# Splitting w_out by half blocks inside the retention, on GpSimd's queue, with two rooms for the samples' keys, values and scores

## The chip, the cores and the metric

The kernel runs on one core of one Trainium2 chip. The metric is the device time of one execution in microseconds (us). A core has five engines with a sequencer each: PE multiplies matrices, DVE (VectorE) and ACT (ScalarE) work on tiles, POOL (GpSimd) does so too, and SP (SyncE) does little but issue transfers. DMA transfers can be issued from SP's, ACT's and POOL's queues. Each engine runs its own instructions in program order; what is ready further back in the row does not overtake.

## The reference, cut to what matters

One step of a hybrid decoder for a prompt of 1024 positions and for 8 samples of 8 positions each. Three branches are made from one normed input, gated, merged and multiplied by `w_out`:

```python
z = rms_norm(x, gain) @ w_in
o_a, s_ret_new = retention(rq, rk, rv, s_ret, pos0)           # 4 heads, chunks of 128 positions
b_a = (silu(rg) * o_a) @ w_br_a
o_b, pool_new = pool_mix(pu, pool_buf, pos0, w_pool, pool_scale)
b_b = (silu(pg) * o_b) @ w_br_b
o_c = nsa_attention(nq, cmp, sel, win, ...)                   # paged rows, window rows, compressed rows
b_c = (silu(ng) * o_c) @ w_br_c
merged = gates[:, :, 0] * b_a + gates[:, :, 1] * b_b + gates[:, :, 2] * b_c
y = x + merged @ w_out
return rms_norm(y, final_gain), new states and cache rows
```

The matmuls take float32 factors as two float16 halves (hi and lo), three products for one. `w_out` (1024x1024 float32, 4 MB) therefore has to be split into hi and lo before its product, which is the last large one of the kernel.

## The kernel before

The work is written as one program for one core, and a scheduler orders each engine's instructions before it runs, by its own timeline of costs; `self.behind()` gives a part lower priority, so that the scheduler lays it into gaps. The stages follow each other: the prompt's projections and attention, to about 520 us; the retention (`retention`), to about 740 us; the samples' attention (`sample_attention`) together with the pooling branch, to about 887 us; the output stage (`output`) with the branch products, the merge and the product with `w_out`, to the end.

**The retention** runs over 36 steps (4 heads by 9 pieces of positions). A step multiplies the input with a block of `w_in` (tile `z`, 24 matmuls of 512 columns), rotates it (`rot`, on DVE), splits it into halves (`rh`: ACT L1259, then the low half on POOL L1260), multiplies (`at`), masks and splits (`am`, then `ah` on ACT L1275 and `al` on DVE L1276), and multiplies again (`ro`, L1328 to L1330). ACT also makes `Sh` (L1347) from the state `S`, `vh` from `z`, `ob` with its row sums `rst`, and `oh`. POOL makes `rst` (L1300, L1301) and the low half of `ga` (L917). A generator of preparatory work for the samples, `prep`, is stepped once a step from the seventh on, behind everything else.

**The samples' attention** runs over four groups `tt` of two samples. For each sample POOL gathers rows of `cache_sel` and `cache_win` into a room `sraw`, ACT and DVE split them into `skd` and `svs`, PE makes scores `s1`, `s2`; DVE and ACT make the softmax in `sS` and `sst`; PE transposes `sS` (`ta` L1089, `tb` L1091), ACT and DVE split that (`sph` L1096, L1098 and `spl` L1097, L1099), PE multiplies with the values (`so`, L1108 and L1111), DVE gathers `soc` (L1114, L1115), PE transposes (`sto`, L1117). The tiles `svs`, `sks`, `sS` and `sst` have one room each, so a group's values and scores take the room of those of the group before.

**The pooling branch** lies between the groups. PE multiplies the input with blocks of `w_in` (tile `pj`, L309 to L311, 384 or 320 columns); ACT takes `pj` (`ue` L1423, `th` L1464), DVE makes `dd`, PE multiplies with `wpl` (`y`, L1467), and DVE and ACT make `gb` (L1468, L1472, L1473), hi and lo of the gated branch. `gb` is the left factor of the output stage's first matmuls `pb` (`branch`, L1642 to L1644).

**The split of w_out** (`out_weights`) is called after the pooling, in a pool of its own. For each of 8 blocks of 128 rows SP issues the load into `wr`, ACT makes `wh` (L222) and DVE makes `wl` (L223), both 128x1024, and SP issues two stores into `wod`, in DRAM. The two halves come from the helper `wsplit`, which also splits `w_in` (tiles `rwh`, `rwl`, `whi`, `wlo`). `wod` is read again only near the end, at 1121 us.

**The output stage** opens by laying rooms `T2`, `T3`, `T4` for factors of a Strassen product, loads them from `txd` and lays `T4a` for the first branch's weights (`store_pair`), which it loads on ACT's queue. The lines that the steps of the prediction turn on, besides those that the difference shows:

```python
with self.behind():
    self.sample_attention(sp, psb, pst)
next(pool, None)
self.out_weights(self.pool(es, "wout"))
...
if n > 5:
    with self.behind():
        next(prep, None)
```

## Time and profile before

| what | value |
|---|---|
| runs of the kernel before | 1311.88, 1307.58, 1310.80 us; median 1310.8 |
| the profiled execution | 1306.29 us; its span 1304.5 us, 1.8 us outside it |
| PE busy | 1251.3 us, 96% of the span |
| DVE, ACT, POOL busy | 912.2, 631.3, 525.2 us |
| matmuls | 10520 |

The span runs from the first to the last instruction that the profile records. A busy share is the time in which an engine worked on an instruction, and an idle stretch of PE is named by the tile it waited for. PEclk is the TensorE clock that was granted, as a share of full speed; it is 1.00 in most stretches and 0.50 in a few. Times of an execution are read on the profiled execution's own scale, which lies 4.5 us under the median of the three runs.

### The profile page before, as it was taken

To read this page: it belongs to the slowest core of one execution; us is meant where nothing else is said; L and a number is where in the kernel's file an instruction comes from. 1 tells how busy PE (TensorE), PEld (TensorE's weight loads), DVE (VectorE), ACT (ScalarE), POOL (GpSimd) and SP (SyncE) were. 2 spreads that over 40 slices of the span, in tenths; PEclk is the share of its full clock that TensorE was granted. 3 is DMA by queue.
4 is the path that set the end of the run, shared out by engine and by line. 5 is a ranking of instruction groups with operands and counts; after the bars stand their busy time and mean duration, and the time that the engine had idled before them with its cause. 6 is when DMAs were issued, how large, how long until landed. Compare 5 with 4: busy or idle time off the path is not lost. (4 is left out here: it accounts for less than half of the span.)

```text
span 1304.5 us, 27795 instructions
## 1 busy us (share of the span) xinstructions
PE 1251.3 (96%) x10520; PEld 850.6 (65%) x10520; DVE 912.2 (70%) x2288; ACT 631.3 (48%) x1474; POOL 525.2 (40%) x561
## 2 busy tenths in 40 slices
PE   7999899989999989999999999999999999999997
PEld 4555566767677764555655565657788888888643
DVE  6648635788777864766766668663698877578975
ACT  5633436667676763555554454433544333213331
POOL 1122013567676751445553550101743566323133
PEclk9999899999999999999999999998999999999998
DMA  7766623698899996243741278327542211543632
GB/s 251 182 133 149 149 66 86 99 147 146 164 173 205 192 207 174 58 124 104 173 139 35 85 202 264 77 76 255 180 130 58 58 49 55 175 145 114 227 96 97
DMA packets 324315, 179.24 MB, mean 137 GB/s; under 512 B 204433, under 2 KB 298609, under 8 KB 323764
## 3 DMA queue, kind: packets, MB, share of 16 engines
q1 hardware_dynamic: 283844, 137.83, 45.3%
q10 hardware_dynamic: 35600, 26.32, 6.8%
q0 software_dynamic: 4736, 13.31, 3.2%
q8 instruction: 82, 1.34, 0.4%
q14 instruction: 53, 0.43, 0.1%
HBM read 98.80 MB, written 33.25 MB: 101 GB/s over the span
## 5 line engine op out<-in xcount | busy, mean ns | idle before, releaser
L761 POOL TENSOR_TENSOR hl<-S,hl 128x640 f16<-128x640 f32 (+7 forms) x128 | 153.8, 1210 | 142.5 <-DVE hl L760 96.6
L309 PE MATMUL pj<-xh,whi 128*128 128x384 f16 (+1 forms) x480 | 153.0, 319 | 2.4 <-ACT ue L1423 2.1
L310 PE MATMUL pj<-xl,whi 128*128 128x384 f16 (+1 forms) x480 | 153.0, 319 | 0.0
L311 PE MATMUL pj<-xh,wlo 128*128 128x384 f16 (+1 forms) x480 | 152.8, 318 | 0.0
L288 PE MATMUL z<-rwh,xh 128*128 128x512 f16 x256 | 97.0, 379 | 0.0
L290 PE MATMUL z<-rwh,xl 128*128 128x512 f16 x256 | 97.0, 379 | 0.0
L289 PE MATMUL z<-rwl,xh 128*128 128x512 f16 x256 | 97.0, 379 | 0.0
L756 ACT ACTIVATE S<-S,nm 128x640 f32<-128x640 f32 (+7 forms) x128 | 93.7, 732 | 5.2 <-DVE hst L852 0.9
L311 PEld LDWEIGHTS <-wlo 128*128 128x128 f16 x672 | 66.1, 98 | 36.6 <-issue 1.3
L310 PEld LDWEIGHTS <-whi 128*128 128x128 f16 x672 | 66.1, 98 | 36.1 <-issue 4.9
L1572 DVE TENSOR_TENSOR q<-st,q 128x288 f32<-128x288 f32 (+1 forms) x168 | 70.3, 433 | 26.4 <-PE st L1563 25.3
L309 PEld LDWEIGHTS <-whi 128*128 128x128 f16 x672 | 66.1, 98 | 33.6 <-issue 1.3
L288 PEld LDWEIGHTS <-xh 128*128 128x128 f16 x448 | 45.3, 101 | 46.4 <-issue 7.2
L290 PEld LDWEIGHTS <-xl 128*128 128x128 f16 x448 | 43.9, 98 | 44.9 <-issue 0.7
L222 ACT ACTIVATE whi<-raw 128x1024 f16<-128x1024 f32 (+1 forms) x48 | 45.5, 948 | 57.0 <-PE pj L310 14.7
L289 PEld LDWEIGHTS <-xh 128*128 128x128 f16 x448 | 43.9, 98 | 42.1 <-issue 0.9
L755 ACT ACTIVATE hl<-S,nm 128x128 f16<-128x128 f32 (+7 forms) x64 | 49.1, 767 | 36.6 <-DMA pt<-hl 36.5
L1328 PE MATMUL o<-vst,pt 128*128 128x64 f16 x528 | 56.3, 193 | 10.7 <-DMA pt<-hl 10.6
L760 DVE CAST hl<-S 128x640 f16<-128x640 f32 (+4 forms) x64 | 33.2, 519 | 45.9 <-ACT S L756 16.2
L1260 POOL TENSOR_TENSOR rh<-rot,rh 128x256 f16<-128x256 f32 (+1 forms) x36 | 26.5, 735 | 89.1 <-ACT rh L1259 88.9
L310 PE MATMUL eg<-xl,whi 128*128 128x384 f16 (+1 forms) x192 | 61.5, 320 | 0.0
L309 PE MATMUL eg<-xh,whi 128*128 128x384 f16 (+1 forms) x192 | 61.5, 320 | 0.0
(511 smaller groups left out, 4056.0 us busy)
## 6 DMA issues: line engine op xcount, KB each, us to landing
raw<-w_in SPq DMA_DIRECT2D x26, 512.0 KB
raw<-w_in ACTq DMA_DIRECT2D x18, 512.0 KB
raw<-w_in SPq DMA_DIRECT2D x48, 128.0 KB
wad<-q ACTq DMA_DIRECT2D x21, 256.0 KB
txd<-rso SPq DMA_DIRECT2D x8, 544.0 KB
raw<-egd SPq DMA_DIRECT2D x16, 272.0 KB
s<-state_ret SPq DMA_DIRECT2D x16, 256.0 KB
o_ret_s<-s POOLq DMA_DIRECT2D x16, 256.0 KB
```

The costliest lines, as they stand in the source:

```text
L222: a = nc.scalar.activation(hi, raw, AF.Copy, scale=WS)
L288: nc.tensor.matmul(out, xh, hi[:, k, c0:c0 + n], start=(k == 0), stop=False)
L289: nc.tensor.matmul(out, xh, lo[:, k, c0:c0 + n], start=False, stop=False)
L290: self.marks["PE"] = nc.tensor.matmul(out, xl, hi[:, k, c0:c0 + n], start=False, stop=(k == 7))
L309: nc.tensor.matmul(out, hi[:, k, :], xh, start=(k == 0), stop=False)
L310: nc.tensor.matmul(out, hi[:, k, :], xl, start=False, stop=False)
L311: self.filled = nc.tensor.matmul(out, lo[:, k, :], xh, start=False, stop=(k == 7))
L755: nc.scalar.activation(hl[:, :w], s[:, d0:c1], AF.Exp, bias=nm[:, br:br + 1], scale=0.125)
L756: nc.scalar.activation(s[:, c0:c1], s[:, c0:c1], AF.Exp, bias=nm[:, br:br + 1], scale=0.125, accum_out=l[:, 0, br, r:r + 1])
L761: nc.gpsimd.tensor_tensor(hl[:, w:2 * w], s[:, d0:c1], hl[:, :w], op=ALU.subtract)
L1328: nc.tensor.matmul(out, lhs[0], rhs[0], start=start, stop=False)
L1572: nc.vector.tensor_tensor(out[:, c0:c0 + n], b, x[:, c0:c0 + n], op=ALU.add)
```

## The change

Three edits.

1. `out_weights` becomes a generator that the retention steps from its seventh step on, next to `prep` and behind everything else. One step issues the load of a block, the next splits it, so a block takes two steps, "half a block" each; the store of block k is issued immediately ahead of the load of block k+1, and the last store behind the eighth block. Loads and stores go on POOL's queue: 8 loads of 512 KB and, hi and lo lying side by side in one room, 8 stores of 512 KB in the place of 16. The rooms are those of the samples' rows, `sraw`, of which there are two and which stand empty in the retention: one holds the float32 block, the other, read as float16, its halves. ACT still makes the high half and DVE the low half. The pool `wout` goes away.
2. `svs`, `sks`, `sS` and `sst` have two rooms each.
3. In the output stage the first room `T4a` is laid ahead of `T2` to `T4`, and the loads of `T3` and `T4` are written behind the second pair's stores; SP's row has them directly behind the load of `T2` as before, and the order of PE's instructions behind the first `pb` is as before.

```diff
@@ -203,7 +203,6 @@
                 with self.behind():
                     self.sample_attention(sp, psb, pst)
                 next(pool, None)
-                self.out_weights(self.pool(es, "wout"))
         with ExitStack() as es:
             self.output(es)
         right.close()
@@ -1013,10 +1012,13 @@
         self.nc.gpsimd.indirect_dma_start(out=out, out_offset=None, in_=rows,
                                           in_offset=bass.IndirectOffsetOnAxis(ap=self.sidx[:, c:c + 1], axis=0))
 
+    def sraw(self, pool):
+        return pool.tile([P, 2, 2, 256], F32, tag="sraw", name=self.nm("sraw"), bufs=2)
+
     def sample_rows(self, pool, b):
 
         nc = self.nc
-        raw = pool.tile([P, 2, 2, 256], F32, tag="sraw", name=self.nm("sraw"), bufs=2)
+        raw = self.sraw(pool)
         for pg in range(2):
             self.gather(raw[:, pg, 0, :], "cache_sel", b * 2 + pg)
         nc.gpsimd.dma_start(raw[:, :, 1, :], self.d["cache_win"][0, b].rearrange("(q p) a g c -> p q (a g c)", p=P))
@@ -1034,8 +1036,8 @@
             for b in range(2):
                 bb = 2 * tt + b
                 raws.append(self.raw0[b] if tt == 0 else self.sample_rows(self.smc if tt == 2 else sp, bb))
-            vs = sp.tile([P, 2, 2, 2, 2, 2, 64], F16, tag="svs", name=self.nm("svs"))
-            ks = sp.tile([P, 2, 8, P], F16, tag="sks", name=self.nm("sks"))
+            vs = sp.tile([P, 2, 2, 2, 2, 2, 64], F16, tag="svs", name=self.nm("svs"), bufs=2)
+            ks = sp.tile([P, 2, 8, P], F16, tag="sks", name=self.nm("sks"), bufs=2)
             for b in range(2):
                 kd = sp.tile([P, 4, 2, 2, 64], F16, tag="skd", name=self.nm("skd"))
                 vo = vs[:, b].rearrange("p q r g a c -> p (q r) g a c")
@@ -1061,8 +1063,8 @@
                                                  tile_position=tp, **fl)
                             kn = self.kns[kr, br * 2 + g] if br < 2 else kcs[kr, g]
                             nc.tensor.matmul(s2[r, br, :], q, kn, tile_position=tp, **fl)
-            s = sp.tile([P, 704], F32, tag="sS", name=self.nm("sS"))
-            st = sp.tile([P, 24], F32, tag="sst", name=self.nm("sst"))
+            s = sp.tile([P, 704], F32, tag="sS", name=self.nm("sS"), bufs=2)
+            st = sp.tile([P, 24], F32, tag="sst", name=self.nm("sst"), bufs=2)
             for br in range(2):
                 nc.vector.tensor_tensor_reduce(out=s[:, br * 256:br * 256 + 256], in0=s1[:, br], in1=tcs, scale=1.0,
                                                scalar=LOW, op0=ALU.add, op1=ALU.max, accum_out=st[:, br:br + 1])
@@ -1162,7 +1164,7 @@
         nc.vector.memset(am, 0.0)
         env = (rope, mt, mts, rv, c2, seq16, qm, am, lg)
         steps = [(h, t) for h in range(4) for t in (0, 1, 2, 3, 8, 4, 5, 6, 7)]
-        prep = self.sample_prep(rp, psa)
+        prep, wout = self.sample_prep(rp, psa), self.out_weights()
         live = []
         for n in range(len(steps) + NSTAGE):
             z = None
@@ -1181,6 +1183,7 @@
             if n > 5:
                 with self.behind():
                     next(prep, None)
+                    next(wout, None)
             if n == len(steps) - 2:
                 with self.behind():
                     self.raw0 = [self.sample_rows(self.smc, b) for b in range(2)]
@@ -1501,17 +1504,23 @@
             self.wsplit(t[:, 0, :n], t[:, 1, :n], a)
             yield i, t[:, :, :n].rearrange("p a (k c) -> p a k c", c=P)
 
-    def out_weights(self, pool):
+    def out_weights(self):
+
 
         nc = self.nc
         self.wod = self.dr.tile([P, 8, 2, 1024], F16, name="wod")
-        for k in range(8):
-            raw = pool.tile([P, 1024], F32, tag="wr", name=self.nm("wr"), bufs=2)
-            nc.sync.dma_start(raw, self.d["w_out"][0][k * P:(k + 1) * P, :])
-            hl = [pool.tile([P, 1024], F16, tag="w" + x, name=self.nm("w" + x), bufs=n) for x, n in (("h", 2), ("l", 1))]
-            self.wsplit(*hl, raw)
-            for a in range(2):
-                nc.sync.dma_start(self.wod[:, k, a], hl[a])
+        hl = None
+        for k in range(9):
+            if hl is not None:
+                nc.gpsimd.dma_start(self.wod[:, k - 1], hl.rearrange("p (a c) -> p a c", a=2))
+            if k == 8:
+                return
+            raw, out = [self.sraw(self.smc).rearrange("p a b c -> p (a b c)") for _ in range(2)]
+            nc.gpsimd.dma_start(raw, self.d["w_out"][0][k * P:(k + 1) * P, :])
+            yield
+            hl = out.bitcast(F16)
+            self.wsplit(hl[:, :1024], hl[:, 1024:], raw)
+            yield
 
     def store_pair(self, wq, i, c0, c1, raw):
 
@@ -1658,11 +1667,12 @@
             wk = self.pool(e, "mwk", bufs=2)
             room = lambda p, tag, kh: p.tile([P, 2, kh, H], F16, tag=tag, name=self.nm(tag), bufs=1)
             xs = (self.xh, self.xl)
+
+            first = room(wk, "T4a", 4)
             tx = {x: room(wk, x, 4) for x in ("T2", "T3", "T4")}
             for a, x in enumerate(xs):
                 nc.sync.dma_start(x[:, 0:4, H:], self.txd[:, 0, a])
-            for i, x in ((2, "T2"), (1, "T3"), (3, "T4")):
-                nc.sync.dma_start(tx[x], self.txd[:, i])
+            nc.sync.dma_start(tx["T2"], self.txd[:, 2])
             rx = self.factors(lambda k, t, c0, n: [x[:, k, t * H + c0:t * H + c0 + n] for x in xs], 4, tx)
             jobs = [(w, C_MG + br * 1024, p) for br in (1, 2) for p in pairs] + [(d["w_br_a"][0], 0, pairs[0])]
             loads = chain((self.load_pair(wk, x, *[c + j * P for j in p]) for x, c, p in jobs),
@@ -1689,8 +1699,12 @@
                 if p == pairs[2]:
                     state.update(A=dict(next(loads)), more=iter(()))
                 if p < pairs[-1]:
-                    x = room(wk, "T4a", 4).rearrange("p a k c -> p (a k c)").bitcast(F32)
+                    x = first if p == pairs[0] else room(wk, "T4a", 4)
+                    x = x.rearrange("p a k c -> p (a k c)").bitcast(F32)
                     self.store_pair(wk, p[0], *[j * P + P for j in p], [x[:, o:o + 1024] for o in (0, 1024)])
+                if p == pairs[1]:
+                    for i, x in ((1, "T3"), (3, "T4")):
+                        nc.sync.dma_start(tx[x], self.txd[:, i])
                 for i, j in enumerate(p):
                     for s0, n in ((0, 352), (352, 192), (544, 352), (896, 192)):
                         pb = self.branch(ps, wb, lambda q: (self.gb, q), range(4 * i, 4 * i + 4), s0, n)
```

The following pieces show where that moves instructions. The names end in numbers of the build; L-numbers are lines of the kernel before or of the changed one, which lie some lines apart (L1259 of before is L1262 of the changed kernel).

PE at the seam from the samples' attention to the output stage, before: `so` and `sto` are the last group's products and transpose, `pb` are the output stage's first matmuls.

```order
L1108 MATMUL so_12055<-vcs,sph_12047 32x128
L1111 LDWEIGHTS spl_12048
L1111 MATMUL so_12055<-vcs,spl_12048 32x64
L1117 MATMUL sto_12107<-ident,soc_12104 128x128
L1642 LDWEIGHTS whi_12857
L1642 MATMUL pb_12905<-gb,whi_12857 128x352
```

The same seam in the changed kernel; `pj` is the pooling branch's last tile:

```order
L308 MATMUL pj_12773<-xh,whi_12703 128x320
L309 LDWEIGHTS whi_12703
L309 MATMUL pj_12773<-xl,whi_12703 128x320
L310 LDWEIGHTS wlo_12704
L310 MATMUL pj_12773<-xh,wlo_12704 128x320
L1470 MATMUL y_12801<-dd_12591,wpl 128x320
L1119 MATMUL sto_12156<-ident,soc_12153 128x128
L1651 LDWEIGHTS whi_12836
L1651 MATMUL pb_12883<-gb,whi_12836 128x352
```

Before, the last group's `ta`, `so`, `tb` and `sto` stand behind the last `pj`, with no other matmul among them. In the changed kernel the last `so` stands ahead of 22 matmuls of the last `pj`, and between that group's `ta`, `tb` and `so` stand further matmuls of `pj`; only `y` and `sto` are left between the last `pj` and the first `pb`.

ACT in the retention, before; `oh`, `ga`, `vh`, `ah`, `rh` and `Sh` are tiles of the retention's steps:

```order
L1304 ACTIVATE oh_8304<-ob_8201,rst_8200 128x256
L916 CAST ga<-to_8212 128x2x4x32
L1239 ACTIVATE rope<-rope,rv 128x1024 x2
L1250 ACTIVATE vh_8353<-z_8232 128x256
L1275 CAST ah_8277<-am_8275 128x128
L1259 CAST rh_8357<-rot_8348 128x256
```

The same place in the changed kernel:

```order
L1307 ACTIVATE oh_8310<-ob_8205,rst_8204 128x256
L915 CAST ga<-to_8216 128x2x4x32
L221 ACTIVATE sraw_8103<-sraw_8102 128x1024
L1242 ACTIVATE rope<-rope,rv 128x1024 x2
L1253 ACTIVATE vh_8363<-z_8238 128x256
L1278 CAST ah_8283<-am_8281 128x128
L1262 CAST rh_8367<-rot_8358 128x256
```

The split of a block (`sraw<-sraw`) now stands among these, eight times over, each 9 to 13 instructions of ACT behind the place at which the block's load was issued; before, the eight stood in ACT's row of the samples' stage, between `ue`, `skd` and `whi`.

POOL in the retention of the changed kernel; `wod<-sraw` is a store and `sraw<-w_out` a load:

```order
L1263 TENSOR_TENSOR rh_8367<-rot_8358,rh_8367 128x256
L916 TENSOR_TENSOR ga<-to_8315,ga 128x2x4x32
L1515 DMA wod<-sraw_8103 128x2048
L1519 DMA sraw_8330<-w_out 128x1024
L1303 TENSOR_TENSOR rst_8303<-rst_8303,half 128x1
L1304 TENSOR_TENSOR rst_8303<-rst_8303,rv 128x1
```

Such a pair of issues stands seven times in POOL's row, between the parts of the steps, with one load ahead of them and one store behind. SP's row loses 24 issues.

## Rows read from the trace of the kernel before

**Rows 1.** The page: its span, and busy time and share of each engine.

```profile
span 1304.5 us, 27795 instructions
...
PE 1251.3 (96%) x10520; PEld 850.6 (65%) x10520; DVE 912.2 (70%) x2288; ACT 631.3 (48%) x1474; POOL 525.2 (40%) x561
```

**Rows 2.** Busy time by stretches (clock and DMA share last).

```profile
core 0: us, PE busy (x) PEld busy (x) DVE busy (x) ACT busy (x) POOL busy (x), PEclk, DMA share, GB/s
545.00:660.00 115.00, 111.12 (x749) 64.18 (x744) 81.53 (x239) 64.14 (x180) 58.14 (x83) 1.00 0.52 135
...
790.00:800.00 10.00, 8.23 (x49) 5.07 (x47) 9.32 (x29) 6.19 (x16) 0.00 (x0) 1.00 0.84 263
...
870.00:881.10 11.10, 8.40 (x54) 5.43 (x52) 8.99 (x26) 5.25 (x16) 0.00 (x0) 1.00 0.35 106
881.10:891.30 10.20, 9.26 (x65) 6.00 (x64) 3.85 (x13) 2.61 (x7) 0.00 (x0) 0.50 1.02 387
...
900.00:1240.00 340.00, 339.53 (x2990) 276.18 (x2988) 263.79 (x459) 127.50 (x248) 142.85 (x109) 1.00 0.39 123
```

**Rows 3.** PE's waits from 740 to 900: total, times, longest.

```profile
PE pj L309 <- ACT ue L1423: 2.1, 1, 2.1
PE so L1108 <- ACT sph L1096: 1.5, 1, 1.5
PE tb L1091 <- DVE spl L1097: 1.2, 1, 1.2
```

**Rows 4.** PE's timeline at the seam: start, duration, instruction, wait.

```profile
876.57 0.30 PE L311 MATMUL pj<-xh,wlo 128*128 128x320 f16 x1
...
887.36 0.50 PE L1642 MATMUL pb<-gb,whi 128*128 128x352 f16 x1
887.65 0.50 PE L1643 MATMUL pb<-gb,whi 128*128 128x352 f16 x1
...
892.11 0.31 PE L1642 MATMUL pb<-gb,whi 128*128 128x352 f16 x1
892.25 0.31 PE L1643 MATMUL pb<-gb,whi 128*128 128x352 f16 x1
```

**Rows 5.** ACT's timeline about 798 us.

```profile
798.82 1.06 ACT L222 ACTIVATE wh<-wr 128x1024 f16<-128x1024 f32 x1 [1.17 <-DMA wr<-w_out]
799.79 0.47 ACT L1423 ACTIVATE ue<-pj 128x384 f32<-128x384 f32 x1
```

**Rows 6.** ACT's and DVE's timelines behind the last pj.

```profile
881.41 0.46 ACT L1472 CAST gb<-th 128x320 f16<-128x320 f32 x1
...
880.64 0.54 DVE L1468 SCALAR_TENSOR_TENSOR th<-y,psc,th 128x320 f32<-128x320 f32 x1
...
881.91 0.49 DVE L1473 TENSOR_TENSOR gb<-th,gb 128x320 f16<-128x320 f32 x1
```

**Rows 7.** Tile wr: w_out's split, and its engines' waits (us, times).

```profile
L222 ACT ACTIVATE wh<-wr x8: 1057/1057/1058, 768.9 to 807.1; 128x1024 f16<-128x1024 f32 x8
L223 DVE SCALAR_TENSOR_TENSOR wl<-wr,wh x8: 1205/1221/1226, 771.4 to 808.4; 128x1024 f16<-128x1024 f32 x8
...
  DMA wr<-w_out: 11.8, 6
```

**Rows 8.** PE's waits in the retention, 520 to 740.

```profile
PE ro L1328 <- ACT Sh L1347: 1.8, 1, 1.8
PE ro L1330 <- DVE al L1276: 1.5, 3, 0.7
PE ro L1328 <- ACT ah L1275: 1.0, 3, 0.4
```

**Rows 9.** ACT's longest waits in the retention, 545 to 665.

```profile
ACT oh L1304 <- POOL rst L1301: 19.9, 14, 2.6
```

**Rows 10.** POOL's issues into sraw (tile sraw), and stretch 770 to 790.

```profile
L1022 POOL DMA_DIRECT2D sraw<-cache_win x8: 773/777/802, 743.2 to 826.5; - x8
...
770.00:790.00 20.00, 20.00 (x159) 12.42 (x158) 19.46 (x39) 7.47 (x12) 10.12 (x9) 1.00 1.05 310
```

## Prediction

> **What bounds the kernel now.** I read the page's engine line first: PE is busy 1251.3 of 1304.5 us [rows 1], so the end moves only where PE's idle time or PE's speed moves. Then I read the stretches around the change [rows 2]. In the retention (545 to 660) PE idles 3.9 of 115 us; ACT is busy for 64.1, DVE for 81.5, POOL for 58.1. In the output stage (900 to 1240) PE idles 0.5 of 340. Between them three stretches stand out. In 790 to 800 PE idles 1.77 of 10 us. In 870 to 881.1 it idles 2.70. In 881.1 to 891.3 it idles 0.94, and the granted clock is 0.50, the lower of its two levels (1.2 against 2.4 GHz), so its 9.26 busy us are some 4.63 us of work at full speed.
>
> PE's waits in those stages name three causes [rows 3]: `pj` for ACT's `ue`, 2.1 us; `so` for ACT's `sph`, 1.5; `tb` for DVE's `spl`, 1.2. The timelines say what stands behind them. The last `pj` matmul starts at 876.57 and the first `pb` at 887.36, and at the seam the `pb` matmuls follow each other at 0.29 us, at 892.11 already without that stretching [rows 4]: the 1.47 and 1.23 us of idling come directly ahead of the fall of the clock. They are there because nothing else is left for PE to do while ACT and DVE make the last group's `sph` and `spl`. And ahead of the late `ue` ACT stood 1.17 us for the DMA of a `w_out` block and then split it for 1.06 us [rows 5]: that wait of 2.1 us is a cost of the split in its old place.
>
> **The change part by part.**
>
> *The seam.* In the new order the last group's `ta`, `tb` and `so` stand ahead of 22 matmuls of `pj` or between other `pj` matmuls, so the answers of ACT and DVE come while PE works. What goes: 2.70 us idle in 870 to 881.1, 0.94 idle in 881.1 to 891.3, and 9.26 / 2 = 4.63 us of lost clock, since with nothing idle ahead the clock has no cause to fall [rows 2]. Together 8.27 us. I put this down to the two rooms of `svs`, `sks`, `sS` and `sst`: without them the last group could not begin early. What is late next: the third group of `pb` (columns 544 on) needs the last piece of `gb`. That chain runs from the end of the last `pj`, 876.57 + 0.30 = 876.87, over `th` and `gb` on ACT and DVE to 881.91 + 0.49 = 882.40: 5.5 us [rows 4, 6]. Before, the products and the transpose covered it. Now `y`, `sto` and the first two groups of `pb` do. These last took 887.36 to 892.11, 4.75 us, most of it at half clock [rows 4]; at full clock I estimate 2.75, and with some 0.75 us for `y` and `sto` 3.5. But the old chain queued on ACT and DVE behind `sph`, `spl` and a block of weights. Its own steps are five of about half a microsecond (0.46, 0.54, 0.49 in [rows 6]), with hand-overs of up to 0.2 us between them (`th` ends at 881.18, `gb` starts at 881.41), so 2.4 to 3.5 us. The wait lies between 0 and 5.5 - 3.5 = 2.0 us; as the order still leaves one block's split among the steps, I take 0.35.
>
> *The split leaves the samples' stage.* Eight ACT instructions of 1057 ns and eight DVE instructions of 1221 ns go from there, with 11.8 us of ACT's standing for `wr` in six waits [rows 7]. Of all this PE felt one wait, 2.1 us [rows 3]; that is the gain. The 24 SP issues that go cost PE nothing, since no wait of PE there names them.
>
> *The split comes into the retention.* ACT gets 8 x 1.06 = 8.5 us, DVE 8 x 1.22 = 9.8 us [rows 7], in sixteen steps or some 100 us. On the stretch 545 to 660 that makes ACT 72.6 and DVE 91.3 of 115 us, 63 and 79%: there is room, and it costs nothing where the work slides into gaps. If the cover is gone, each split delays `ah`, `al` or `Sh`, for which PE already waits 1.0, 1.5 and 1.8 us [rows 8]. The bound from below is zero, or little more. The bound from above is that every block costs what the one at 798 us cost, 8 x 2.1 = 16.8 us, since a block is load wait plus split there too. The nearest row is the samples' stage as a whole, where eight such blocks cost PE 2.1 us [rows 3]; the retention hands over between engines more often, and I take 3 us. The order puts a split 9 to 13 ACT instructions, about one step of 6 us, behind its load's issue; the ACT waits for `wr` averaged 11.8 / 6 = 1.97 us at a DMA share of 0.84 [rows 2, 7], while the retention's stretch has 0.52. Loads of 4 MB and stores of 4 MB in 100 us add about 84 GB/s to 135, by which the share would come to some 0.84; `w_in`'s blocks come over the same engines, and later ones would show as ACT waiting for `raw`.
>
> *POOL's queue.* Eight loads and eight stores at the duration of a plain issue there, 0.78 us [rows 10], are 12.5 us; POOL goes from 58.1 to some 70.6 of 115 [rows 2]. Behind a store or load stand `rst`, the low half of `rh` and of `ga`. ACT's `oh` already waits 19.9 us in 14 waits for `rst` [rows 9], and none of PE's waits names `oh`, so a POOL some tenths later per step reaches PE only over the low half of `rh`, which precedes `at`. I book it within the 3 us. A store waits for both halves of its own block, made a step earlier; the loads behind it wait with it.
>
> *T4a first, T3 and T4 later in the text.* SP's and PE's rows keep their order there; the output stage from 900 on idles 0.5 of 340 us [rows 2], so I cost this at nothing. If `T4a` first moved the branch's weights earlier, PE still has no wait to lose.
>
> **The sum.** 8.27 + 2.1 - 0.35 - 3.0 = 7.0 us. The profiled execution took 1306.3 us, so 1299.3 on its own scale; the median of the three runs shown lies 4.5 above it, 1310.8, so the forecast is **1303.8 us**.
>
> **The rivals.**
>
> *The retention hides the split wholly.* ACT and DVE have more than a third and more than a fifth of the stretch free. Then the 3 us fall away: 1300.8.
>
> *The seam idles again, further on.* The chain to `gb` stays as long as it was, PE stands 2.0 us ahead of the third group of `pb`, and the clock falls as it did behind the 2.70 us. That takes 2.0 + 4.63 from the gain instead of 0.35: 10.4 - 6.6 - 3.0 = 0.8, 1310.0 us. For it speaks that the order leaves little between the last `pj` and `pb`; against it that PE's idling at 798 us, 2.1 us at one time, left the clock of its stretch at 1.00 [rows 2, 3].
>
> *The splits hold up the retention (slower).* ACT stands in its row for a block that is not yet there, and `ah`, `rh` and `Sh` stand behind it. At the price of the block at 798 us, 2.1 each [rows 3, 5], the change loses 16.8 and gains 10.0: 1317.6 us. It turns the sign from 10.0 / 8 = 1.25 us a block and is measurable from 1.74. For it speaks that ACT stood for six of eight blocks before [rows 7]; against it the step's distance of load and split, and a DMA share of 0.52.
>
> *POOL stalls on its issues.* Were an issue held for the length of a DVE instruction, up to 1.22 us [rows 7], sixteen would add 19.5 us to POOL; half of it on PE's path gives 9.8 us, 1310.6 us. Against it: while DVE was busy 19.46 of 20 us (770 to 790), issues of the samples' windows took 773 to 802 ns, hardly spread [rows 10]. The Trainium skill has the rule that speaks for this rival, under "SBUF — State Buffer", section "SBUF: two separate sides": descriptors of a DMA issued from GpSimd are written over a port pair that VectorE can hold locked, so that the transfer waits for the end of VectorE's instruction. In this trace the narrow spread does not bear it out for such issues.
>
> **How the numbers follow.** Chances: the forecast 0.50 (its own range 1300 to 1308), nothing lost in the retention 0.18, the seam again 0.15, the retention held up 0.12, POOL 0.05. A difference of 0.3%, 3.9 us, is about what a measurement of this kernel can tell from none, so faster means under 1306.9 and slower over 1314.7. Faster: 0.44 of the first (the upper end of its range lies within 0.3%), 0.18, and 0.02 of the milder form of the seam, 0.64. Same: the rest of the first 0.06, the seam 0.13, POOL 0.05, 0.24. Slower: 0.12. The range is 1299 to 1312: below it lies little, since the sum with nothing lost anywhere is 10.4; above it the held up retention.
>
> **What would show the steps right or wrong.** Right: PE's waits name no `so<-sph`, no `tb<-spl`, and no `pj<-ue` of 2 us, and the first `pb` follow at 0.15 us with a granted clock of 1.00. The split's ACT instructions lie between about 560 and 680 us, with short waits for the DMA. Wrong: a wait of over a microsecond ahead of `pb`, with the clock at 0.50 behind it; or PE's waits in the retention of well over 5 + 3 us, by `ah`, `al`, `rh` or `Sh`, with ACT standing for `sraw<-w_out`, or POOL's DMA issues taking over a microsecond. The prediction fails above all if the price of a block in the retention is not the 0.4 us that I took.

## The result, and the profile after

The changed kernel takes 1321.38 us in the median of 4 runs (1320.78 to 1322.44), the kernel before 1310.99 (4 runs): a ratio of 1.0086, with a 95% interval from 1.0062 to 1.011. It is slower, by some 10 us, where 1303.8 was forecast and 1312 was the upper end of the range. The profiled execution took 1321.12 us.

The page's span and engine line, which answer to [rows 1]:

```profile
span 1319.3 us, 27777 instructions
...
PE 1253.8 (95%) x10520; PEld 850.7 (64%) x10520; DVE 914.0 (69%) x2288; ACT 630.4 (48%) x1474; POOL 530.7 (40%) x577
```

PE does the same matmuls; 14.8 us more of span hold 2.5 more of busy time. To see where the rest lies I read five marks off PE's timeline in either trace (where the first `z`, the last `ro`, the first matmul of the third group of `pb`, the first `st` and the first `py` start; `st` and `py` are matmuls of the output stage), and took the stretches between them:

| stretch, us | before | after | difference |
|---|---|---|---|
| start to first `z` (code untouched) | 498.4 | 500.3 | +1.9 |
| first `z` to last `ro` (retention) | 257.5 | 267.8 | +10.3 |
| last `ro` to third group of `pb` (samples, seam) | 136.2 | 133.6 | -2.6 |
| third group of `pb` to first `st` (output's beginning) | 41.7 | 47.6 | +5.9 |
| first `st` to first `py` | 278.8 | 280.0 | +1.2 |
| first `py` to the span's end | 91.9 | 90.1 | -1.8 |

The first row is noise: over the thirteen profiled executions of this study that untouched stretch ran from 497.2 to 503.9 us. The last two rows nearly cancel. Three rows carry the result, and each went against the forecast: the retention lost over three times what was booked, the samples' stage gave back a quarter of the gain that was forecast for it, and the output stage, booked at nothing, lost 5.9.

**The retention.** PE's waits there, from 500 to 760 us (total, times, longest), against [rows 8]:

```profile
PE ro L1331 <- ACT ah L1278: 3.4, 1, 3.4
PE cms L989 <- DMA craw<-cache_cmp,idx: 2.2, 1, 2.2
...
PE ro L1331 <- ACT Sh L1350: 1.7, 1, 1.7
PE ro L1333 <- DVE al L1279: 1.4, 2, 1.1
```

ACT's waits for transfers, from 545 to 700 us:

```profile
ACT rwh L221 <- DMA raw<-w_in: 10.8, 6, 3.8
...
ACT sraw L221 <- DMA sraw<-w_out: 7.5, 4, 3.2
ACT whi L221 <- DMA raw<-w_in: 4.7, 2, 3.2
```

ACT's timeline through the longest of PE's waits, which ends in the `ro` of 587.81 us:

```profile
577.89 0.63 ACT L221 ACTIVATE rwh<-raw 128x512 f16<-128x512 f32 x1 [3.71 <-DMA raw<-w_in]
...
580.16 1.06 ACT L221 ACTIVATE sraw<-sraw 128x1024 f16<-128x1024 f32 x1
...
581.37 1.68 ACT L221 ACTIVATE rwh<-raw 128x512 f16<-128x512 f32 x3
...
586.93 0.63 ACT L221 ACTIVATE rwh<-raw 128x512 f16<-128x512 f32 x1 [1.42 <-DMA raw<-w_in]
587.47 0.28 ACT L1278 CAST ah<-am 128x128 f16<-128x128 f32 x1
```

The point of these rows is that `ah` stands in ACT's row directly behind `rwh`, the split of a piece of `w_in` (256 KB, brought by two loads of 128 KB), and that it is `rwh` that waits, for its own loads: 1.42 us here, 3.71 at the piece of 577.89. The wait for `w_out` itself (`sraw`) is there too, but it is not what stands ahead of this `ah`. What went out just ahead of that late piece are a store and a load of `w_out`, POOL's timeline, then SP's:

```profile
571.29 0.60 POOL L1515 DMA_DIRECT2D wod<-sraw  x1
571.88 0.54 POOL L1519 DMA_DIRECT2D sraw<-w_out  x1
```

```profile
572.80 0.55 SPq L274 DMA_DIRECT2D raw<-w_in  x1
```

The piece was used 5.1 us after this issue. Pieces of `w_in` come in only two bursts of eight in this window (issued from 565 to 584 and from 634 to 651 us), and a pair of `w_out` transfers meets each of them: in the second burst the pair went out at 635.22 and 635.82, and the piece issued at 636.37 was used 7.1 us later. In the kernel before, the pieces that ACT stood for were used 2.4 to 3.4 us after their issue. Step by step, by the starts of the `at` matmuls counted from the first `z`, the changed kernel is level with the one before up to the first burst, 3.3 us late behind it, 5.8 behind the wait for a gather (`cms`, at 629.8 us) and 10.3 behind the second burst; after that it loses nothing more. The loss has three places, not eight; at two of them it follows a late piece of `w_in`.

Busy time by stretches, with the granted clock ahead of the DMA share:

```profile
545.00:660.00 115.00, 104.94 (x700) 59.98 (x699) 79.52 (x225) 62.12 (x167) 59.64 (x91) 0.98 0.65 176
580.00:600.00 20.00, 16.61 (x128) 10.49 (x127) 14.04 (x34) 12.75 (x33) 11.63 (x17) 0.91 0.45 123
```

In 545 to 660 PE now idles 10.1 us where it idled 3.9 [rows 2], the DMA share is 0.65 against 0.52, and behind the wait of 3.4 us the clock fell to its lower level for some 3.5 us (0.91 in the mean of these twenty), and once more at 659.9 us; before, it was 1.00 throughout the retention.

**The samples' stage.** PE's waits from 760 to 920 us, against [rows 3]:

```profile
PE pt L1437 <- DVE tl L1434: 1.5, 1, 1.5
...
PE pb L1651 <- ACT gb L1475: 1.2, 1, 1.2
PE so L1110 <- ACT sph L1098: 0.9, 1, 0.9
PE ptb L1431 <- DVE win L1448: 0.5, 1, 0.5
PE tb L1093 <- DVE spl L1099: 0.5, 1, 0.5
```

The waits of [rows 3] at the seam and for `ue` are gone, and the clock is 1.00 where the first `pb` run. But new ones stand at other groups of samples, and `pb` waits 1.2 us for `gb`.

**The output's beginning.** ACT's timeline:

```profile
901.21 1.09 ACTq L1492 DMA_DIRECT2D T4a<-w_br_a  x2
...
914.60 1.15 ACT L221 ACTIVATE q<-T4a 128x512 f16<-128x512 f32 x2 [10.12 <-DMA T4a<-w_br_a]
915.65 0.30 ACT L1712 COPY mm<-pb 128x192 f32<-128x192 f32 x1
```

SP's timeline at the same time:

```profile
900.55 0.34 SPq L1675 DMA_DIRECT2D T<-txd  x1
901.14 0.81 SPq L1707 DMA_DIRECT2D T<-txd  x2
```

The same in the kernel before, ACT's timeline, then SP's:

```profile
888.44 1.02 ACTq L1489 DMA_DIRECT2D T4a<-w_br_a  x2
...
894.15 1.15 ACT L222 ACTIVATE q<-T4a 128x512 f16<-128x512 f32 x2 [1.53 <-DMA T4a<-w_br_a]
```

```profile
881.25 1.29 SPq L1665 DMA_DIRECT2D T<-txd  x3
```

Before, the three loads of `T` (1088 KB each) had 7.2 us of start over `T4a`, and `T4a` was used 5.7 us after its issue. Now they go out within the same microsecond and `T4a` is used 13.4 us after its issue. ACT stands for it 10.1 us, with the copies of `mm` behind it, and PE waits for `mm` from there on:

```profile
PE pb L1651 <- ACT mm L1712: 4.5, 6, 1.2
PE st L1570 <- ACT mm L1712: 1.6, 2, 0.9
PE pb L1651 <- ACT gb L1475: 1.2, 1, 1.2
```

(PE's waits from 900 to 960 us.) The kernel before has none of the first two, but for 0.5 us at one `st`. The time from the first load of `T` to the use of `T4a` hardly changed: 12.9 us before, 14.1 now. The 7 us in which PE idled and ran at half clock at the seam before were also the time in which that burst of loads was under way.

### The profile page after: what moved, and what is told of

Its sections match the earlier page's. It is cut to its first block, busy times and chain, and to the rows that moved or that the text cites. A ratio compares the mean times of both kernels' runs of the same rounds, so it can differ in the third digit from the quotient of the medians.

```text
span 1319.3 us, 27777 instructions
## 1 busy us (share of the span) xinstructions
PE 1253.8 (95%) x10520; PEld 850.7 (64%) x10520; DVE 914.0 (69%) x2288; ACT 630.4 (48%) x1474; POOL 530.7 (40%) x577
```

## The experiments

The theory after the traces: three separate costs. In the retention the transfers of `w_out` make the blocks of `w_in` late, and ACT's row passes that on; in the samples' stage the second rooms let a group's products move ahead of their factors; in the output stage `T4a` shares the DMA engines with the `T` loads. The rivals for the retention: the split's own work on ACT and DVE; ACT's standing for a block of `w_out`; POOL's queue. The table has each kernel's median, its ratio to the kernel before on the same chip with its interval, and three of the stretches from its profiled execution.

| kernel | median us | ratio | retention | samples, seam | output's beginning |
|---|---|---|---|---|---|
| before | | | 257.5 | 136.2 | 41.7 |
| the change | 1321.4 | 1.0086 [1.0062, 1.011] | 267.8 | 133.6 | 47.6 |
| e1, no split | 1313.3 | 1.0038 [1.0013, 1.0063] | 257.9 | 132.0 | 48.4 |
| e2, the work only | 1312.9 | 1.0030 [1.0013, 1.0046] | 257.9 | 132.7 | 48.4 |
| e3, the transfers only | 1321.6 | 1.0105 [1.0080, 1.0131] | 260.4 | 132.4 | 48.5 |
| e10, the same again | 1322.4 | 1.0079 [1.0052, 1.0105] | 265.5 | 130.8 | 48.4 |
| e4, the move only | 1324.7 | 1.0125 [1.0103, 1.0146] | 269.1 | 127.6 | 48.9 |
| e5, T4a first on SP | 1320.5 | 1.0053 [1.0031, 1.0075] | 269.8 | 134.0 | 43.2 |
| e6, no split, one room | 1308.8 | 0.9983 [0.9967, 1.0000] | 256.4 | 128.1 | 48.3 |
| e7, slow pace | 1312.1 | 1.0007 [0.9987, 1.0028] | 258.1 | 132.5 | 48.8 |
| e8, split late, one room | 1305.4 | 0.9952 [0.9931, 0.9973] | 258.6 | 128.9 | 43.4 |
| e9, slow pace, one room | 1306.5 | 0.9962 [0.9942, 0.9982] | 257.5 | 127.9 | 43.2 |
| e11, on SP's queue | 1320.2 | 1.0069 [1.0045, 1.0093] | 263.9 | 134.0 | 48.9 |

**e1, the change without the split.**

```diff
     def out_weights(self):
-        for k in range(9):
...
+        yield
...
-                    nc.sync.dma_start(wo[a][:, k], self.wod[:, k, a])
+                    nc.sync.dma_start(wo[a][:, k], self.txd.rearrange("p a b c d -> p (a b c d)")[:, k * 2048 + a * 1024:][:, :1024])
```

> The changed kernel without the split of w_out: no load, no split, no store of it (its halves are read from another array of halves, so y is not the reference's y); the two rooms and T4a first stay. The stretch from the first z matmul to the last ro matmul took 257.5 us before and 267.7 us after. If the split's presence is what holds up the retention, it falls back to 257 to 260 and the time to about 1311. If the rest of the new order does it (the scheduler's different row, or the profiled run itself), it stays over 264 and the time over 1317. In both cases the output stage keeps its new waits of pb and st for mm, some 6 us, if these come from the seam's new order and not from the split's transfers; if they come from those, they are gone and the time is about 1306.

The retention is back at 257.9 us: the split's presence made the loss there. The median, 1313.3, is 2 us over what was expected. The output's beginning stays at 48.4, so its new waits don't come from the split's transfers; that they come from the seam's order and not from edit 3 is for e4 to show. And without any split of `w_out` at all this kernel is still slower than the one before.

**e2 and e3, the work and the transfers apart.**

In e2:

```diff
-        for k in range(9):
...
+        raw, out = [self.sraw(self.smc).rearrange("p a b c -> p (a b c)") for _ in range(2)]
+        self.nc.gpsimd.dma_start(raw, self.d["w_out"][0][0:P, :])
+        hl = out.bitcast(F16)
+        for k in range(8):
+            yield
+            self.wsplit(hl[:, :1024], hl[:, 1024:], raw)
+            yield
```

In e3, where `wod` holds float32:

```diff
-            hl = out.bitcast(F16)
-            self.wsplit(hl[:, :1024], hl[:, 1024:], raw)
+            hl = raw
```

> The changed kernel with one load of w_out in the place of eight and no store; the eight splits on ACT and DVE stand in the retention as they did, all on the same block (halves for the product are read from another array, so y is not the reference's y). If the work itself (8 x 1.06 us on ACT, 8 x 1.22 us on DVE) holds up the retention, first z to last ro stays at 265 to 268 us. If the wait for the block's transfer or the transfers do it, it falls to 257 to 261.

> The changed kernel with the eight loads and eight stores on POOL's queue in the retention, but with no split: the store takes the block as it was loaded (halves for the product are read from another array, so y is not the reference's y). If the transfers alone hold up the retention (later blocks of w_in, later gathers behind them on POOL's queue), first z to last ro stays at 265 to 268 us. If ACT's standing in its row for a block, or the split's work, does it, it falls to 257 to 261.

The work alone costs nothing: 257.9 us and a median within half a microsecond of e1's. Eight instructions of 1.06 us on ACT and eight of 1.22 on DVE did slide into gaps. The transfers alone bring the median to 1321.6, which is the change's own. The profiled execution of e3 showed only 260.4, though; it was the fastest of its four (1315.1 us). So it was run again:

> The kernel with the transfers of w_out in the retention and no split, once more, since its profiled execution (1315.1 us, first z to last ro 260.4) was its fastest and its median 1321.6. If the transfers alone hold up the retention as much as the whole change, the median is again over 1319 and a profiled execution of that length shows 264 to 268 us. If the transfers cost only part and the rest is ACT's standing for a block of w_out, the median is 1314 to 1318 and the stretch 259 to 263.

The median was again over 1319, 1322.4, and the stretch 265.5. ACT's waits for transfers in e10, from 545 to 700 us:

```profile
ACT rwh L221 <- DMA raw<-w_in: 12.2, 8, 3.8
...
ACT whi L221 <- DMA raw<-w_in: 5.7, 3, 3.9
```

The same lines in e2:

```profile
ACT rwh L221 <- DMA raw<-w_in: 6.9, 7, 2.0
...
ACT whi L221 <- DMA raw<-w_in: 1.1, 1, 1.1
```

ACT's waits for blocks of `w_in` go from 8.0 us to 17.9 (15.1 in e3) when the transfers of `w_out` are there. With no split of `w_out` in ACT's row the ratio is already the change's, within the intervals; ACT's standing for `w_out`, 7.5 us in the change, adds nothing that the medians show. How long the same transfers hold PE up differs by the execution: in e3's, PE's two longest waits in the retention were 2.1 and 1.8 us and the clock stayed at 1.00; in e10's they were 4.1 and 3.2 us, and the clock fell at both (0.83 in the mean of 580 to 600, 0.86 in 660 to 680). Both waits stand behind the two bursts there too.

**e11, the same transfers on SP's queue.**

```diff
-            nc.gpsimd.dma_start(raw, self.d["w_out"][0][k * P:(k + 1) * P, :])
+            nc.sync.dma_start(raw, self.d["w_out"][0][k * P:(k + 1) * P, :])
...
-                nc.gpsimd.dma_start(self.wod[:, k - 1], hl.rearrange("p (a c) -> p a c", a=2))
+                nc.sync.dma_start(self.wod[:, k - 1], hl.rearrange("p (a c) -> p a c", a=2))
```

> The changed kernel with the eight loads and eight stores issued on SP's queue, at the same places, in the place of POOL's. If the loss in the retention comes over POOL's queue (the issues' own time there, gathers of cache_cmp and rst behind them), first z to last ro falls from 267.7 to 258 to 262 us. If it comes from the transfers meeting the blocks of w_in, whichever queue issues them, it stays at 264 or more; on SP's queue they stand in one row with the loads of w_in, so it may grow.

The stretch is 263.9, between the two bounds but at the edge of the second, and within the 260.4 to 269.8 of the five kernels that have these transfers at this pace on POOL's queue. The time stays at 1320.2, so POOL's queue is not the main cause. ACT's waits of `rwh` are as long as they ever were:

```profile
ACT rwh L221 <- DMA raw<-w_in: 13.3, 7, 3.3
```

What did go is the wait of `cms` for a gather, 2.2 us in the change and of which e11's rows have nothing. But e3 and e10, with the same sixteen issues on POOL's queue, don't have it either, so that it came over that queue is not shown.

**e7, half the pace.**

```diff
             if n > 5:
                 with self.behind():
                     next(prep, None)
+            if n > 3 and n % 2 == 0:
+                with self.behind():
                     next(wout, None)
```

> The changed kernel with a half block every second step of the retention, from the fifth step on, in the place of one every step: the same loads, stores and splits, spread over twice the time, and two steps between a block's load and its split. If the retention is held up by transfers that meet the blocks of w_in, in bursts, first z to last ro falls from 267.7 to 259 to 263 us and the time to 1313 to 1317. If each block has its price wherever it stands, it stays over 265 and the time at 1320 or more, or the loss moves into the samples' stage.

258.1 us: the loss in the retention is gone with the same loads, stores and splits, and the time is 1312.1, both a little under what was expected. ACT's waits for `w_in`, 545 to 700 us:

```profile
ACT whi L221 <- DMA raw<-w_in: 4.9, 3, 2.4
...
ACT rwh L221 <- DMA raw<-w_in: 2.4, 4, 1.2
```

The longest wait of `rwh`, 3.8 us in the change, is 1.2, and no row of that stretch has ACT waiting for `sraw`. So a block has no fixed price. But e7 changes two things at once, the pace and the places. Its pairs went out at 561.0, 588.4, 615.4 and 643.7 us, and the bursts of `w_in` pieces from 566 to 582 and from 627 to 641 lie between them (POOL's timeline, then SP's):

```profile
561.57 0.57 POOL L1521 DMA_DIRECT2D sraw<-w_out  x1
...
588.42 0.60 POOL L1517 DMA_DIRECT2D wod<-sraw  x1
```

```profile
566.07 1.47 SPq L273 DMA_DIRECT2D raw<-w_in  x1
...
581.46 0.46 SPq L274 DMA_DIRECT2D raw<-w_in  x1
```

The pieces that ACT stood for were used 2.3 to 3.3 us after their issue, much as in the kernel before. The pair of 643.7 went out beside three whole blocks of `w_in` (512 KB each, for `whi`); ACT's wait for these is 4.9 us, against 2.4 before, and the retention shows no loss from it. In all six kernels at full pace (the change, e3, e4, e5, e10, e11) the load of a pair went out 0.5 to 1.3 us ahead of a piece in each burst, and that piece was used 4.3 to 8.2 us after its issue. So the traces speak more for the place of a pair, just ahead of or within a burst, than for the pace; no run moves the pairs at one pace, and the two are not parted.

**e4, the move alone.**

Against the changed kernel, `T4a` is laid as before, and the four tiles of the samples have one room again:

```diff
-            vs = sp.tile([P, 2, 2, 2, 2, 2, 64], F16, tag="svs", name=self.nm("svs"), bufs=2)
-            ks = sp.tile([P, 2, 8, P], F16, tag="sks", name=self.nm("sks"), bufs=2)
+            vs = sp.tile([P, 2, 2, 2, 2, 2, 64], F16, tag="svs", name=self.nm("svs"))
+            ks = sp.tile([P, 2, 8, P], F16, tag="sks", name=self.nm("sks"))
...
-            s = sp.tile([P, 704], F32, tag="sS", name=self.nm("sS"), bufs=2)
-            st = sp.tile([P, 24], F32, tag="sst", name=self.nm("sst"), bufs=2)
+            s = sp.tile([P, 704], F32, tag="sS", name=self.nm("sS"))
+            st = sp.tile([P, 24], F32, tag="sst", name=self.nm("sst"))
```

> The kernel before with the move of w_out's split alone: one room for svs, sks, sS and sst, T4a laid as before. Its row of PE already has the last so ahead of the last pj. If the move is what opened the seam, the waits of so and tb of 1.5 and 1.2 us and the half clock at the seam are gone here too, the output stage has its waits for mm, and the time is within 3 us of the changed kernel's 1321.4. If the two rooms opened it, the seam idles as before, the waits for mm are absent and the time is about 1310.8 - 2.1 + 10 = 1319 with first z to last ro at 266 to 268 us.

The first branch of the expectation came true: the seam is open with one room. From 768 to 903 us PE's waits are this one row:

```profile
PE pb L1651 <- ACT gb L1475: 1.2, 1, 1.2
```

and the stretch is 127.6 us, 8.6 under the kernel before. So the move opened the seam, and the second rooms did not. The time, 1324.7, lies 3.3 us over the change's, where at most 3 were expected. Two rooms beside the split in its old place were not tried. e4 also leaves edit 3 out, and its output's beginning takes 48.9 us, with ACT standing 10.5 us for `T4a`: that loss comes from the seam's new order, not from edit 3.

**e6, one room, without the split.**

> As the kernel without the split of w_out, and with one room for svs, sks, sS and sst (halves for the product are read from another array, so y is not the reference's y). From the last ro to the third group of pb the kernel before took 136.2 us, the one without the split and with two rooms 132.0, the one with the move alone and one room 127.6. If the second rooms cost those 4 to 5 us (the group's ptb, y, so and tb come earlier in PE's row than their factors), the stretch falls to 126.5 to 129 and the time from 1313.3 to about 1309. If they don't, it stays at 131 to 133 and the time at 1313.

The edit is that of e4 upon e1. The stretch fell to 128.1 and the median to 1308.8, as expected to 0.3 us. PE's waits from 757 to 895 us in e1, with two rooms:

```profile
PE pb L1637 <- ACT gb L1475: 1.2, 1, 1.2
PE so L1110 <- ACT sph L1098: 0.9, 1, 0.9
PE ptb L1431 <- DVE os L1438: 0.5, 1, 0.5
PE tb L1093 <- DVE spl L1099: 0.5, 1, 0.5
PE y L1470 <- DVE os L1438: 0.4, 1, 0.4
```

With one room only the first of these is left, and 0.2 us of `s`. The second rooms cost 3.9 us: 2.3 us of waits, and a stretch of 3.4 us at the lower clock behind them, which costs half of its length. With them, by the names in the waits, a group's products stand earlier in PE's row, where their factors are not ready.

**e5, T4a ahead of the T loads.**

```diff
-            for a, x in enumerate(xs):
-                nc.sync.dma_start(x[:, 0:4, H:], self.txd[:, 0, a])
-            nc.sync.dma_start(tx["T2"], self.txd[:, 2])
...
-                if p == pairs[1]:
-                    for i, x in ((1, "T3"), (3, "T4")):
-                        nc.sync.dma_start(tx[x], self.txd[:, i])
+                if p == pairs[0]:
+                    with self.tc.issue_after(self.loaded.ins):
+                        for a, x in enumerate(xs):
+                            nc.sync.dma_start(x[:, 0:4, H:], self.txd[:, 0, a])
+                        for i, x in ((2, "T2"), (1, "T3"), (3, "T4")):
+                            nc.sync.dma_start(tx[x], self.txd[:, i])
```

`self.loaded` is there the load of the first `T4a`, for which `load_pair` now gets `nc.sync`.

> The changed kernel, with the first load of T4a (w_br_a, 2 x 512 KB) issued on SP's queue ahead of the loads of xh, xl, T2, T3 and T4, which follow it there, in the place of ACT's queue behind the cast of gb. In the changed kernel T4a landed some 13 us after its issue, among 3.3 MB of T loads, ACT stood 10.1 us for it, and PE's waits of pb and st for mm came to 6 us. If that burst is the cause, ACT's wait for T4a falls under 4 us, the stretch from the third group of pb to the first st goes from 47.5 to 41.5 to 43 us and the time from 1321.4 to about 1316. If mm is late for what ACT does itself (the splits q ahead of mm in its row), stretch and time stay within 1.5 us of the changed kernel's.

ACT's wait for `T4a`, 895 to 960 us:

```profile
ACT q L221 <- DMA T4a<-w_br_a: 6.3, 3, 3.2
```

The longest wait is 3.2 where it was 10.1, the three together 6.3 (under 4 was expected), and the stretch 43.2 us where it was 47.6. The stretch shows the gain; the time does not: about 1316 was expected, the median is 1320.5, and the ratio of 1.0053 against 1.0086 lies within overlapping intervals. In the profile this kernel's retention took 269.8, 2.0 more than the change's. The edit moves `T4a` to another queue as well as ahead of the other loads; the two are not parted.

**e8 and e9, two ways to mend it.** Both have one room and e5's order. e9 keeps the split in the retention at e7's pace; e8 splits `w_out` only in the output stage, straight into the tiles of the last product:

```diff
-            for a in range(2):
-                for k in range(8):
-                    nc.sync.dma_start(wo[a][:, k], self.wod[:, k, a])
+            for k in range(8):
+                r = self.wtile([P, 1024], F32, "raw")
+                nc.sync.dma_start(r, d["w_out"][0][k * P:(k + 1) * P, :])
+                self.wsplit(wo[0][:, k], wo[1][:, k], r)
```

> All of the kernel before but the place of the split, and the seam as it should be: one room for svs, sks, sS and sst; T4a's first load ahead of the T loads on SP's queue; and w_out split in the output stage, at about 1120 to 1160 us, straight into the two tiles that the last product reads, with no store into wod and no load from it. The sum by the theory of three places: the retention back to 257.5, the samples' stage 127.6 to the third pb against 136.2, the output's first stretch 42 against 41.7: 8 us under the kernel before, 1301 to 1304. If eight splits of 1.06 and 1.22 us hold up DVE before the last product (it is busy 20 of 40 us at 1120 to 1160, but 18 of 20 from 1160 on), PE's wait of py for tb grows from 1.9 to over 5 us and the time is 1306 or more.

> The change's own idea mended at its three places: a half block every second step of the retention, one room for svs, sks, sS and sst, and T4a's first load ahead of the T loads on SP's queue. Worked out from the runs so far: 1312.1 (slow pace alone), less 4.4 us for the one room (132.0 to 128.2 from the last ro to the third pb, and 1313.3 to 1308.75), less 4.4 us for T4a's place (51.7 to 47.3 from the first pb to the first st): 1303.3, faster than the kernel before by 0.4 to 0.6%. If the three costs share waits, so that mending one already gave part of the others, it is 1306 to 1309.

Both beat the kernel before: 0.9952 [0.9931, 0.9973] and 0.9962 [0.9942, 0.9982]. Their medians, 1305.4 and 1306.5, are 5.2 and 4.4 us under the kernel before. They lie 1.4 us above the expected range of the one and 3.2 above the sum of the other, so the three costs don't quite add up when mended together. In e9 the pairs missed the bursts of `w_in` pieces, as in e7. e8's feared wait did not grow; from 900 to 1260 us:

```profile
PE py L1842 <- DVE tb L222: 1.9, 1, 1.9
PE pb L1637 <- ACT mm L1698: 1.3, 1, 1.3
```

In e9 PE's waits from 520 to 960 us come to some 8 us, less than those of the change from 520 to 760 alone (10.9):

```profile
PE ro L1333 <- ACT Sh L1352: 1.9, 1, 1.9
PE ro L1333 <- ACT ah L1280: 1.3, 3, 0.6
PE pb L1653 <- ACT gb L1477: 1.2, 1, 1.2
```

## Why the prediction was wrong

**The split in the retention: the step that failed.** The prediction booked 3 us, with 0 and 16.8 as bounds. The stretch took 10.3 more, 1.29 us a block in the mean, just past the 1.25 us at which by the slower rival the sign turns. The bounds held; the value was taken from the wrong row, and a price by the block was the wrong measure, since the loss stands at three places and not at each of the eight blocks. One of the prediction's own signs of being wrong came: PE's waits from 520 to 760 us are 10.9 us, over its 5 + 3. The split was priced by the work and by ACT's standing for its block, as in the samples' stage. But the work costs nothing (e2), and what costs is the transfers of `w_out` that go out beside the loads of `w_in` (e3, e10), which the prediction saw ("later ones would show as ACT waiting for `raw`") and gave no price. In the samples' stage of the kernel before, ACT's waits from 755 to 887 us name no block of `w_in`, though `w_out` went out there too; so that row had nothing of this cost in it. The slower rival had the right place and engine, `ah` behind ACT's row, and the wrong block: the row stood for `w_in`, not mainly for `w_out`. That the same eight blocks can go through the retention without a loss, e7 shows; whether by their pace or by where they fall against `w_in`'s bursts stays open, and the issue times speak for the second.

**The seam.** The size was right and the cause wrong. 10.0 us were forecast for seam and `ue` together; with one room the stretch gives 8.6 (e4). The second rooms, to which the prediction put the gain down, take 3.9 of it away (e1 against e6), and in the changed kernel 2.6 is left; of the 2.1 between, 1.5 is its wait of `pt` for `tl`, which e1's rows don't have. That they could cost anything stood nowhere in the prediction. The wait of `pb` for `gb` is 1.2 us in every kernel with the new seam, not 0.35: in the changed kernel DVE's row still has the low half of a weight block, 1.23 us at 898.57, ahead of that `th`. The rival of an idling seam did not come: the clock stayed at 1.00 there.

**The output stage: booked at nothing.** "PE still has no wait to lose" read the stretch from 900 on as it was, with the `T` loads already under way. In both kernels SP's row has loads of `T` that wait for the last `th` (all three before, the last two now); shortening the time between that and the first use of `T4a` took the cover away. Price: 5.9 us, of which e5 gives back 4.4.

**POOL's queue.** The rival of stalled issues did not come true. In the trace of the changed kernel the issues of `w_out` on POOL, by tile `sraw` (min, median, max ns), are

```profile
L1519 POOL DMA_DIRECT2D sraw<-w_out x8: 542/572/620, 543.7 to 654.6; - x8
...
L1515 POOL DMA_DIRECT2D wod<-sraw x8: 577/601/612, 559.7 to 677.7; - x8
```

hardly spread, shorter than the 0.78 us that was taken, with DVE 69% busy in 545 to 660. The rule in the Trainium skill, "SBUF — State Buffer", section "SBUF: two separate sides", speaks of VectorE's instructions in a two-port mode; no row here tells the mode of an instruction, so these durations show that the issues were not held, and not that the rule is wrong. e11, with no such issue, was no faster than its interval can tell.

**The sum.** Forecast: 3.0 - 10.0 + 0 = -7.0. By stretches: 10.3 - 2.6 + 5.9 = 13.6, with +1.9 ahead of it and -0.6 behind 14.9, the span's 14.8 up to rounding. The medians differ by 10.4, since the profiled execution of before lies 4.7 under its median and that of after at it.

What stays open: how much of the retention's loss is the loads and how much the stores, which were not parted; whether the pace of the pairs or their place decides; and whether POOL's queue has a share, such as the 2.2 us at a gather.

## What to carry to other kernels

Work that is moved into a busy stage is priced by its transfers too: look for the loads with the shortest lead over the bound engine in that stage, and ask what they become when a store and a load of 512 KB go out just ahead of them. Compare issue times before taking an average price for each piece of work. Before an idle stretch is removed, look at which transfers run in it; they need their time elsewhere, and the first that the next stage uses should be issued first. A second room gave the scheduler freedom here, not time: when products move ahead, look at whether their factors come earlier as well.

## What the runs showed of the hardware

A load of 2 x 512 KB was in use 5.7 us after its issue when 3.3 MB had been issued 7.2 us ahead of it, 13.4 us after its issue when they were issued in the same microsecond, and 5.5 us after its issue when it went out ahead of them (e5). A piece of `w_in`, 256 KB by two loads, was used 2.3 to 3.4 us after its issue where ACT stood for it in the kernel before and in e7; it took 5.1 and 7.1 us in the change, where a store and a load of 512 KB each had gone out directly ahead, the load under 1 us before. And the same program's first 500 us, which no kernel changes, ran from 497.2 to 503.9 us over thirteen profiled executions, more than most differences here: stretches tell more than single times.
